# A two-mixer transformer layer on one core: five modulation groups in front, the context ahead of two gates, four modulation quarters brought forward

## The chip, the cores and the metric

The kernel runs as one program on one core of a Trainium2 chip. The metric is the device time of one execution in microseconds (us), the median of several runs. TensorE (PE) does the matrix products and transposes, VectorE (DVE) and ScalarE (ACT) the elementwise work, GpSimd (POOL) and SyncE (SP) mostly issue transfers. Each engine works through its own instructions in the order in which the program puts them; a semaphore holds an instruction back until what it reads is there and what it overwrites is free.

## What is computed

One layer over 512 latent tokens and 256 context tokens of width 1024, all in float32. What matters here is its beginning:

```python
m_lat = silu(c) @ mod_w + mod_b          # 6 sections of 1024: sh1, sc1, g1, sh2, sc2, g2
m_ctx = silu(c_ctx) @ mod_w + mod_b
h_lat = rms_norm(x,   norm_mix_g) * (1 + sc1)  + sh1
h_ctx = rms_norm(ctx, norm_mix_g) * (1 + csc1) + csh1
...
z_lat, z_ctx = h_lat @ w_in, h_ctx @ w_in   # qkv, decay and beta columns, gates g_a, g_b, m_a, m_b
...
x = x + g1 * ((sigmoid(m_a) * ya + sigmoid(m_b) * yb) @ w_out)
x = x + g2 * swiglu(rms_norm(x, norm_ffn_g) * (1 + sc2) + sh2)
```

Between the two places stand two token mixers (a gated delta rule and HGRN2), each run in both directions over context and latent tokens in chunks of 64. The front of the kernel, on which the change lies, makes `h_lat` and `h_ctx`, 8 of the 24 gate tiles, and the decay columns.

## The kernel before

**Products.** Each float32 operand is split in a high and a low part of a rounded type: `split` loads a weight tile `raw`, ScalarE writes `hi` (L100), VectorE writes `lo` (L102). A product is three matmuls, high by high, low by high and high by low (`mm3`, L110). `hhi`, `hlo` hold `h_lat` so, transposed (8 feature tiles of 128 features by 512 tokens), `chi`, `clo` hold `h_ctx` (by 256 tokens).

**The front, stage by stage** (all of it inside the pool `s1`). SP loads four tiles of x, then the first two sections of `mod_w`, 8 MB, as eight tiles `mw` of 1 MB (a ring of six buffers); after each two of them come two tiles `wr`, the weights of six gates for one feature tile, 384 KB each; then the two context tiles. Rows of x are normed (`norm_rows`, ACT L264, DVE L270).

- `modulation(q)`, q = 0 to 3, makes shift and scale of two feature tiles: PE multiplies the two `mw` tiles into `pmod` (L279, 16 matmuls in strips of 32 rows), DVE copies it to `mr` (L282), PE adds the strips and turns rows into columns with `comb` (L284, 128x2 matmuls), DVE adds biases into `mcol` (L291 to L293).
- `prepare(d)` calls `normed(d, 0, ...)`: PE transposes x into `px` (L299), ACT writes `hhi` (L301) and the unrounded `hf` (L303), DVE `hlo` (L304). Around it ACT writes `wh` (L313) and DVE `wl` (L315), the split of `wr`; they use the ring of two buffers that `hi` and `lo` use.
- Then 18 matmuls per feature tile (L330), 144 in all, add up the six gates 16 to 21 in six banks of PSUM, the accumulator memory of PE, named `pg` in the rows.
- `gate_out` copies a gate to `gt` (ACT, L136, two buffers) and writes it to memory (`gdram`, on SP). Gates 22 and 23 follow as ordinary products (`pgate`, 48 matmuls), then the eight context tiles (`normed(d, 1, ...)`, in the three PSUM banks of the tag "ga"), then small columns and the mask `lev`, loaded as float32 and cast by ACT (L346).
- The next block (pool `s3`) multiplies both streams by the decay columns (`pab`, L375), copies to `abT` (L376), transposes back (L379), and runs a row of some 25 small DVE steps from `ab` (L381) to `la` (L412), which PE sums into `pg` (L419) and ACT turns into `dec` (L422).

**The planner.** Everything after that comes from generators that emit work in the order of a string, `PLAN`: `H0` to `H3` and `G0`, `G2` are the parts of the two mixers, `F` emits one of the remaining gates, `N` and `aT` call `mod_early`. That function makes one quarter (256 columns) of one of the last three sections needed for `g1`, `sh2`, `sc2`: a transfer of 1 MB into a tile `mwe` on POOL's queue (L847), two multiplications (L851), six multiply-adds (L853), one addition (L854) on DVE, eight matmuls that sum the columns into `pmo` (L116), and an addition into `vc` (L862). Seven of the twelve are emitted so; four of these stand near the start of `PLAN`. In the rows, `h_z` are H0's projections, `g_k_zl`, `g_k_zc`, `g_q_zl`, `g_v_zl`, `g_v_zc` those of G0.

**What orders the instructions.** A scheduler places each instruction by a priority that counts up in program order; work emitted at a raised `tc.cur_priority` is filled in where the engine would otherwise stand. The resulting order on each engine is fixed when the program is built.

## Time and profile before

| | |
|---|---|
| median of 3 runs | 1079.61 us (1078.65 to 1081.12) |
| the profiled execution | 1081.61 us, its span 1079.6 us |
| granted PE clock, mean | 0.99 |
| time from the start to the end of the 144 gate matmuls | 70.4 us |
| time to the first matmul of G0 | 104.5 us |
| transfers | 122.07 MB, mean 113 GB/s |

The profile shows one execution. A row of a timeline reads: start, duration, engine, line, operation, what it writes and reads, shapes, number of instructions; in brackets stand the idle time of that engine just before it and what ended it. Durations of matmuls overlap, since the next one starts before the last has drained, so what one costs is read from the distance of starts.

### The profile page before, as it was taken

How to read it: one execution, taken by the hardware profiler on the slowest of the kernel's cores; microseconds unless marked ns; L12 is line 12 of the kernel's file. 1: busy time of each engine (PE TensorE's matmuls, PEld its weight loads, DVE VectorE, ACT ScalarE, POOL GpSimd, SP SyncE). 2: the span in 40 equal slices, each digit the busy share in tenths (PEclk: the TensorE clock that was granted, in tenths of full speed). 3: DMA queues.
4: the chain of work that ended last, by engine and by line, in shares of the span. 5: the costliest groups of instructions: out<-in, count | busy, mean ns of one | idle time of the engine just before them, and what ended most of it. 6: DMA issues, size and time to landing. Idle time of an engine off the chain costs nothing.

```text
span 1079.6 us, 16501 instructions
## 1 busy us (share of the span) xinstructions
PE 1014.1 (94%) x6455; PEld 839.9 (78%) x6455; DVE 656.5 (61%) x1238; ACT 554.5 (51%) x1042; POOL 76.6 (7%) x133
## 2 busy tenths in 40 slices
PE   4999999979999999999999899999999999999996
PEld 2686788858897877789777688797888878888785
DVE  3336886789867967976797565776343433422524
ACT  3456578748976765887774643442222222221212
POOL 1010000320002022000201000010000000000000
PEclk8999999999999999999999999999999999999999
DMA  9953412122004213200738743455333323322222
GB/s 329 290 168 91 138 55 65 54 79 59 3 11 147 64 45 88 59 2 22 241 112 280 239 159 120 137 158 174 98 97 96 96 85 98 97 97 96 86 95 95
DMA packets 134529, 122.07 MB, mean 113 GB/s; under 512 B 5533, under 2 KB 110259, under 8 KB 134451
## 3 DMA queue, kind: packets, MB, share of 16 engines
q1 hardware_dynamic: 127715, 100.20, 29.9%
q0 software_dynamic: 4640, 17.30, 4.9%
q10 hardware_dynamic: 2096, 3.50, 0.9%
q8 instruction: 51, 0.84, 0.3%
q14 instruction: 27, 0.22, 0.1%
HBM read 110.51 MB, written 10.49 MB: 112 GB/s over the span
## 4 chain that ended last, share of the span: by engine, by line
PE 60%; DVE 13%; DMA 9%; ACT 7%; issue 7%; POOL 3%; SPq 0%; POOLq 0%; ACTq 0%; DVEq 0%
PE pf L110 20%; PE pfo L110 10%; PE pg L330 3%; PE pup L110 3%; PE h_z L110 3%; PE pgate L110 2%; DMA mwb<-in_mod_w_dram 2%; DVE lo L102 2%; DMA mwe<-in_mod_w_dram 2%; PE h_zv L110 2%; DMA ug<-gdram 1%; ACT hi L100 1%; DMA gdram<-gt 1%; PE p_s_pk L801 1%; PE g_k_zl L110 1%
## 5 line engine op out<-in xcount | busy, mean ns | idle before, releaser
L100 ACT CAST hi<-raw 128x1024 fp32r<-128x1024 f32 (+1 forms) x131 | 129.7, 991 | 279.9 <-PE pf L110 97.3
L102 DVE TENSOR_TENSOR lo<-raw,hi 128x1024 fp32r<-128x1024 f32 (+1 forms) x131 | 150.5, 1150 | 172.6 <-ACT hi L100 172.2
L110 PE MATMUL pf<-hhi,lo 128*128 128x512 f32 (+1 forms) x352 | 133.8, 380 | 0.8 <-DVE lo L102 0.8
L110 PE MATMUL pf<-hhi,hi 128*128 128x512 f32 (+1 forms) x352 | 133.8, 381 | 0.0
L110 PE MATMUL pf<-hlo,hi 128*128 128x512 f32 (+1 forms) x352 | 133.7, 380 | 0.0
L110 PEld LDWEIGHTS pf<-hhi,lo 128*128 128x128 f32 x352 | 66.2, 188 | 13.7 <-DVE lo L102 1.2
L110 PEld LDWEIGHTS pf<-hlo,hi 128*128 128x128 f32 x352 | 66.2, 188 | 12.5 <-DVE hlo L1042 0.2
L110 PEld LDWEIGHTS pf<-hhi,hi 128*128 128x128 f32 x352 | 66.1, 188 | 12.5
L110 PE MATMUL pfo<-lo,uh 128*128 128x512 f32 x176 | 68.8, 391 | 0.1
L110 PE MATMUL pfo<-hi,ul 128*128 128x512 f32 x176 | 68.5, 389 | 0.0
L110 PE MATMUL pfo<-hi,uh 128*128 128x512 f32 x176 | 67.9, 390 | 0.0
L110 PE MATMUL pgate<-hhi,lo 128*128 128x512 f32 x144 | 59.2, 412 | 6.5 <-DVE lo L102 6.5
L110 PE MATMUL pgate<-hhi,hi 128*128 128x512 f32 x144 | 59.2, 411 | 2.3 <-ACT hi L100 2.3
L110 PE MATMUL pgate<-hlo,hi 128*128 128x512 f32 x144 | 58.2, 404 | 0.0
L1098 DVE TENSOR_TENSOR sg<-sg,pf 128x512 f32<-128x512 f32 x22 | 15.1, 687 | 49.3 <-PE pf L110 49.3
L835 DVE SCALAR_TENSOR_TENSOR acc<-mwb,sc,acc 128x256 f32<-128x256 f32 x72 | 34.5, 484 | 12.4 <-DMA mwb<-in_mod_w_dram 11.2
L110 PEld LDWEIGHTS pfo<-lo,uh 128*128 128x128 f32 x176 | 33.0, 188 | 7.8 <-DVE lo L102 1.0
L110 PEld LDWEIGHTS pfo<-hi,uh 128*128 128x128 f32 x176 | 32.8, 188 | 7.4 <-ACT hi L100 0.7
L110 PEld LDWEIGHTS pgate<-hhi,lo 128*128 128x128 f32 x144 | 27.8, 193 | 13.8 <-DVE lo L102 8.9
L110 PE MATMUL h_z<-hhi,hi 128*128 128x512 f32 x96 | 38.1, 397 | 0.4 <-ACT abT L376 0.3
L110 PEld LDWEIGHTS pfo<-hi,ul 128*128 128x128 f32 x176 | 33.0, 188 | 6.8
L110 PE MATMUL h_z<-hhi,lo 128*128 128x512 f32 x96 | 38.0, 396 | 0.0
(443 smaller groups left out, 2498.3 us busy)
## 6 DMA issues: line engine op xcount, KB each, us to landing
raw<-in_ffn_w_in_dram SPq DMA_DIRECT2D x44, 512.0 KB, 3.7
raw<-in_w_in_dram SPq DMA_DIRECT2D x37, 512.0 KB, 3.7
raw<-in_ffn_w_out_dram SPq DMA_DIRECT2D x22, 512.0 KB, 3.6
mwb<-in_mod_w_dram POOLq DMA_DIRECT2D x18, 512.0 KB, 4.6
mw<-in_mod_w_dram SPq DMA_DIRECT2D x16, 512.0 KB, 6.0
mwe<-in_mod_w_dram POOLq DMA_DIRECT2D x7, 1024.0 KB, 6.1
gdram<-gt SPq DMA_DIRECT2D x24, 256.0 KB, 3.3
...
```

The lines of the kernel that those rows point to most:

```text
L100: nc.scalar.copy(hi[:, :, :], raw[:, :, :])
L102: nc.vector.tensor_tensor(lo[:, :, :], raw[:, :, :], hi.bitcast(F32), op=ALU.subtract)
L110: nc.tensor.matmul(ps, a[u](k), b[v](k), start=(start and n == 0), stop=(stop and n == tot - 1))
L330: nc.tensor.matmul(pg0[i][:, :], u[:, P * i:P * i + P], v[:, d, :], start=(d == 0 and n == 0), stop=(d == KT - 1 and n == 2))
L801: nc.tensor.matmul(pk[:, 2 * P:3 * P], kend[:, :], u[:, :], start=True, stop=True)
L835: nc.vector.scalar_tensor_tensor(acc[:, :], mw[:, k - k0, :], sc[:, k:k + 1], acc[:, :], op0=ALU.mult, op1=ALU.add)
L1098: nc.vector.tensor_tensor(sg[:, :], sg[:, :], pgu[1][:, :], op=ALU.mult)
```

## The change

1. **Five groups.** `modulation` takes a range of feature tiles: (0,1), (1,2), (2,4), (4,6), (6,8). The first two groups need one `mw` tile of 1 MB each (all 1024 rows, 128 columns of each section, so runs of 512 bytes instead of 1 KB). `wr0` is loaded behind the first `mw`, `wr1` behind the second. The column matmuls go in strips of 32 columns (32x2, four times as many).
2. **The context first.** `normed(d, 1)` follows the six gates directly, in the two banks "ha"; of every odd tile `hf` is written by DVE.
3. **Fillers.** Gates 22 and 23 and four quarters (`mwe20` to `mwe23` by the numbers in the rows below) are emitted at a priority raised by 1500. The gates get own tiles `rw` for their high and low parts, the quarters tiles of the ring `mw`, loaded on SP. The four entries at the start of `PLAN` go; the other `N` and `aT` stay and use POOL as before.
4. **Small.** `lev` is passed as bytes (112 KB loaded in place of 448 KB, no cast). `gt` has three buffers in the front.

```diff
-PLAN = ("H0:1 aT:1 N:1 aT:2 G0:6 F:1 H1:3 G0:4 F:1 G2:3 G0:5 F:2 N:1 G0:1 H0:2 "
+PLAN = ("H0:1 G0:6 F:1 H1:3 G0:4 F:1 G2:3 G0:5 F:2 N:1 G0:1 H0:2 "
...
-    return sq, np.concatenate(lev, axis=1).astype(np.float32)
+    return sq, np.concatenate(lev, axis=1).astype(np.uint8)
...
-            gt = pool.tile([P, SEQ], F32, name=f"gt{i}", tag=tag, bufs=2)
+            gt = pool.tile([P, SEQ], F32, name=f"gt{i}", tag=tag, bufs=3 if pool is ring.get("sp") else 2)
...
+        quarters = [(sec, j) for sec in (2, 3, 4) for j in range(4)]
+
+        def mod_now(sec, j, mw, queue):
+
+            c0 = D * sec + 256 * j
+            queue.dma_start(mw[:, 0:KT, :], T["mod_w"][0, :, c0:c0 + 256].rearrange("(k p) f -> p k f", p=P))
+            for k in range(KT):
+                acc = mw[:, k % 2, :]
+                if k < 2:
+                    nc.vector.tensor_scalar_mul(acc, acc, sc[:, k:k + 1])
+                else:
+                    nc.vector.scalar_tensor_tensor(acc, mw[:, k, :], sc[:, k:k + 1], acc, op0=ALU.mult, op1=ALU.add)
+            nc.vector.tensor_tensor(mw[:, 0, :], mw[:, 0, :], mw[:, 1, :], op=ALU.add)
+            mod_sum(sec, j, mw[:, 0, :], "fa")
+
+        def mod_sum(sec, j, acc, tag):
+            ps = bank(tag, f"pmo{sec}{j}")
+            for i in range(2):
+                column_sums(ps, i, acc[:, P * i:P * i + P])
+            c = 8 * sec + 2 * j
+            nc.vector.tensor_tensor(mbc[:, c:c + 2], ps[:, 0:2], mbc[:, c:c + 2], op=ALU.add)
...
+            groups = ((0, 1), (1, 2), (2, 4), (4, 6), (6, 8))
+
+            def load_mod(d0, d1):
+                n, kn = P * (d1 - d0), KT // (d1 - d0)
+                for k0 in range(0, KT, kn):
+                    mw = s1.tile([P, kn, 2 * n], F32, name=f"mw{d0}_{k0}", tag="mw", bufs=6)
+                    for j in range(2):
+                        c0 = D * j + P * d0
+                        nc.sync.dma_start(mw[:, :, n * j:n * j + n],
+                                          T["mod_w"][0, P * k0:P * (k0 + kn), c0:c0 + n].rearrange("(k p) f -> p k f", p=P))
+                    for k in range(kn):
+                        mws.setdefault(d0, []).append(mw[:, k, :])
...
+            wrs = [s1.tile([P, NG0 * P], F32, name="wr0", tag="wr", bufs=5)]
+            for g in (0, 1):
+                xts[g] = s1.tile([P, D], F32, name=f"xt{g}")
+            for d0, d1 in groups:
+                load_mod(d0, d1)
+                for e in range(d0, d1):
+                    wr = wrs.pop() if wrs else s1.tile([P, NG0 * P], F32, name=f"wr{e}", tag="wr", bufs=5)
                     nc.sync.dma_start(wr[:, :], W_IN[P * e:P * e + P, C_MB:C_MB + NG0 * P])
                     wraws.append(wr)
-                if d == 1:
+                if d0 == 1:
...
+            def modulation(d0, d1):
+
+                nd = d1 - d0
+                ps = bank("ha", f"pmod{d0}")
+                for k, mw in enumerate(mws[d0]):
+                    r = slice(32 * (k % 4), 32 * (k % 4) + 32)
+                    nc.tensor.matmul(ps[r, 0:2 * P * nd], sch[:, k, :], mw, start=(k < 4), stop=(k >= 4), tile_position=(0, r.start))
+                mr = s1.tile([P, 512], F32, name=f"mr{d0}", tag="mr", bufs=2)
+                nc.vector.tensor_copy(mr[:, 0:2 * P * nd], ps[:, 0:2 * P * nd])
+                for i in range(2 * nd):
+                    for j in range(0, P, 32):
+                        nc.tensor.matmul(ps[j:j + 32, 2 * i:2 * i + 2], mr[:, P * i + j:P * i + j + 32], comb[:, :],
+                                         start=True, stop=True, tile_position=(0, j))
+                col = ps[:, 0:4 * nd].rearrange("p (j d s) -> p j s d", j=2, s=2)
+                dd = slice(d0, d1)
...
+                if s == 1 and d % 2:
+                    nc.vector.tensor_scalar(hf[:, 0:n], px[:, 0:n], scl, sh, op0=ALU.mult, op1=ALU.add)
+                else:
+                    nc.scalar.activation(hf[:, 0:n], px[:, 0:n], AF.Identity, bias=sh, scale=scl)
...
-            modulation(0)
+            modulation(*groups[0])
             prepare(0)
+            nxt = {0: 1, 1: 2, 2: 3, 4: 4}
             for d in range(KT):
-                if d % 2 == 0 and d + 2 < KT:
-                    modulation(d // 2 + 1)
+                if d in nxt:
+                    modulation(*groups[nxt[d]])
                 if d + 1 < KT:
                     prepare(d + 1)
...
-            for i in rest[0:2]:
-                gate(i, sp)
             for d in range(KT):
-                normed(d, 1, (0, 1), chi, clo, "ga")
+                normed(d, 1, (0, 1), chi, clo, "ha")
...
-            levf = s1.tile([P, 7 * P], F32, name="levf")
-            nc.sync.dma_start(levf[:, :], T["lev"])
-            nc.scalar.copy(lev[:, :], levf[:, :])
+            nc.sync.dma_start(lev[:, :], T["lev"])
...
+            tc.cur_priority += 1500
+            for i in rest[0:2]:
+                w = [s1.tile([P, KT, P], F32R, name=f"rw{i}{j}") for j in range(2)]
+                w = split([W_IN[:, gcols[i]:gcols[i] + P]], KT, P, dst=[t[:, :, :] for t in w])
+                gate_out(i, feat(w, lat, SEQ, f"pgate{i}"), sp, "gt")
+            for q in quarters[0:4]:
+                mod_now(*q, s1.tile([P, KT, 256], F32, name="mwe%d%d" % q, tag="mw", bufs=6), nc.sync)
+            del quarters[0:4]
+            tc.cur_priority -= 1500
...
+            mod_now(sec, j, gd.tile([P, 12 if tag == "N" else KT, 256], F32, name=f"mwe{sec}{j}", tag=tag), nc.gpsimd)
```

The tensors' numbers in the rows that follow tell instances apart (`px01` is feature tile 1 of x, `px12` tile 2 of the context). On PE, around the first gate matmuls, before:

```order
L279 MATMUL pmod0_216<-mw1_117,sch_181 32x512 x4
L299 MATMUL px00_237<-sq_91,xt5_112 128x128
L284 MATMUL pmod0_216<-comb_184,mr0_225 128x2 x4
L330 MATMUL pg0_0_210<-hhi_73,wh0_234 128x512
L330 MATMUL pg0_1_211<-hhi_73,wh0_234 128x512
L330 MATMUL pg0_2_212<-hhi_73,wh0_234 128x512
L330 MATMUL pg0_3_213<-hhi_73,wh0_234 128x512
L330 MATMUL pg0_4_214<-hhi_73,wh0_234 128x512
L330 MATMUL pg0_5_215<-hhi_73,wh0_234 128x512
L330 MATMUL pg0_0_210<-hhi_73,wl0_235 128x512
```

and in the changed kernel:

```order
L315 MATMUL pmod0_216<-comb_184,mr0_225 32x2 x8
L310 MATMUL pmod1_251<-mw1_0_121,sch_181 32x256 x8
L366 MATMUL pg0_0_210<-hhi_73,wh0_238 128x512
L331 MATMUL px01_276<-sq_91,xt2_106 128x128
L331 MATMUL px01_276<-sq_91,xt3_108 128x128
L331 MATMUL px01_276<-sq_91,xt4_110 128x128
L331 MATMUL px01_276<-sq_91,xt5_112 128x128
L315 MATMUL pmod1_251<-comb_184,mr1_260 32x2 x8
L366 MATMUL pg0_1_211<-hhi_73,wh0_238 128x512
L366 MATMUL pg0_2_212<-hhi_73,wh0_238 128x512
```

The first group no longer stands behind `mw1`; the second group's matmuls and the transposes of feature tile 1 now stand ahead of and right behind the first gate matmul.

On ACT, from the first to the fourth feature tile, before:

```order
L301 ACTIVATE hhi_73<-px01_268,mcol_189 128x512
L303 ACTIVATE hf01_274<-px01_268,mcol_189 128x512
L313 CAST wh2_296<-wr2_134 128x768
L301 ACTIVATE hhi_73<-px02_299,mcol_189 128x512
L303 ACTIVATE hf02_305<-px02_299,mcol_189 128x512
L313 CAST wh3_345<-wr3_136 128x768
L301 ACTIVATE hhi_73<-px03_348,mcol_189 128x512
```

and in the changed kernel:

```order
L333 ACTIVATE hhi_73<-px01_276,mcol_189 128x512
L338 ACTIVATE hf01_282<-px01_276,mcol_189 128x512
L348 CAST wh2_334<-wr2_136 128x768
L348 CAST wh3_395<-wr3_138 128x768
L333 ACTIVATE hhi_73<-px02_337,mcol_189 128x512
L338 ACTIVATE hf02_343<-px02_337,mcol_189 128x512
L333 ACTIVATE hhi_73<-px03_398,mcol_189 128x512
```

The cast `wh3` now stands ahead of `hhi` of tile 2, where it stood behind it and `hf`.

On DVE, from the copy `ab2` of the decay columns on, before:

```order
L381 COPY ab2_758<-pab_751 128x192
L388 COPY cw_765<-pr_762 128x60
L383 TENSOR_TENSOR ab_760<-ab2_758 128x96
L390 COPY dta_767<-pr_762 128x16
L241 TENSOR_SCALAR beta_796<-ab_760 128x48
L395 TENSOR_TENSOR zz_772<-ab_760,dta_767 128x48
L393 TENSOR_SCALAR nal_769<-nal_769 128x8
L397 SCALAR_TENSOR_TENSOR e_774<-zz_772 128x48
```

and in the changed kernel:

```order
L424 COPY ab2_902<-pab_895 128x192
L162 TENSOR_SCALAR mwe23_832<-mwe23_832,sc_173 128x256
L426 TENSOR_TENSOR ab_904<-ab2_902 128x96
L162 TENSOR_SCALAR mwe23_832<-mwe23_832,sc_173 128x256
L438 TENSOR_TENSOR zz_916<-ab_904,dta_911 128x48
L271 TENSOR_SCALAR beta_940<-ab_904 128x48
L164 SCALAR_TENSOR_TENSOR mwe23_832<-mwe23_832,sc_173 128x256
L440 SCALAR_TENSOR_TENSOR e_918<-zz_916 128x48
L273 TENSOR_SCALAR beta_940<-beta_940 128x48
L164 SCALAR_TENSOR_TENSOR mwe23_832<-mwe23_832,sc_173 128x256
L443 TENSOR_SCALAR t_921<-e_918 128x48
L452 TENSOR_SCALAR zz_916<-zz_916 128x48
```

Between the small steps that lead to `la` there now stand the eight steps of quarter `mwe23`.

## Rows read from the trace of the kernel before

**Rows 1.** Page, part 1: busy us (share of the span) xinstructions of each engine.

```profile
PE 1014.1 (94%) x6455; PEld 839.9 (78%) x6455; DVE 656.5 (61%) x1238; ACT 554.5 (51%) x1042; POOL 76.6 (7%) x133
```

**Rows 2.** Stretches: us, busy (x) of PE, PEld, DVE, ACT, POOL; clock, DMA share, GB/s.

```profile
20.00:24.00 4.00, 2.58 (x6) 2.10 (x7) 2.05 (x4) 1.45 (x2) 0.00 (x0) 0.50 1.10 358
...
52.00:56.00 4.00, 4.00 (x27) 3.02 (x20) 1.75 (x6) 1.65 (x3) 0.55 (x1) 1.00 0.01 4
```

**Rows 3.** Timeline of PE in the front (columns as told above).

```profile
13.25 1.93 PE L279 MATMUL pmod<-mw,sch 128*32 128x512 f32 x8 [7.43 <-DVE xt L270]
...
16.22 1.20 PE L279 MATMUL pmod<-mw,sch 128*32 128x512 f32 x8 [0.21 <-DMA mw<-in_mod_w_dram]
...
21.42 2.93 PE L330 MATMUL pg<-hhi,wh 128*128 128x512 f32 x6 [2.13 <-ACT hhi L301]
...
27.75 1.06 PE L279 MATMUL pmod<-mw,sch 128*32 128x512 f32 x8
...
30.27 0.97 PE L330 MATMUL pg<-hhi,wh 128*128 128x512 f32 x3 [0.40 <-ACT hhi L301]
...
33.36 0.96 PE L284 MATMUL pmod<-comb,mr 128*128 128x2 f32 x8
...
37.00 1.07 PE L330 MATMUL pg<-hhi,wh 128*128 128x512 f32 x4
...
69.03 1.52 PE L330 MATMUL pg<-hlo,wh 128*128 128x512 f32 x6
```

**Rows 4.** Timeline of ACT in the front.

```profile
34.88 0.78 ACT L301 ACTIVATE hhi<-px,mcol 128x512 fp32r<-128x512 f32 x1 [3.27 <-DVE mcol L293]
...
37.20 0.83 ACT L313 CAST wh<-wr 128x768 fp32r<-128x768 f32 x1 [0.87 <-PE pg L330]
...
74.17 1.24 ACT L136 COPY gt<-pg 128x512 f32<-128x512 f32 x2 [2.52 <-DMA gdram<-gt]
```

**Rows 5.** Timeline of PE, rest gates, context and decay columns.

```profile
70.39 0.39 PE L110 MATMUL pgate<-hhi,hi 128*128 128x512 f32 x1
...
81.28 0.81 PE L299 MATMUL px<-sq,xt 128*128 128x128 f32 x6
...
83.27 0.31 PE L375 MATMUL pab<-chi,wab 128*32 128x256 f32 x1 [1.02 <-ACT chi L301]
...
100.69 0.60 PE L419 MATMUL pg<-la,sq 128*128 128x24 f32 x4
...
104.50 0.40 PE L110 MATMUL g_k_zl<-hhi,hi 128*128 128x512 f32 x1
```

**Rows 6.** Timeline of DVE, the chain from the decay columns to `la`.

```profile
94.71 0.36 DVE L381 COPY ab<-pab 128x192 f32<-128x192 f32 x1 [0.75 <-PE pab L379]
...
100.34 0.20 DVE L412 TENSOR_TENSOR la<-e,nal 128x48 f32<-128x48 f32 x1
```

**Rows 7.** Timeline of PE in G0's projections.

```profile
128.34 0.31 PE L116 MATMUL pmo<-ones,mwe 128*32 128x1 f32 x16 [1.69 <-DVE mwe L854]
...
130.83 0.63 PE L110 MATMUL pgate<-hhi,hi 128*128 128x512 f32 x1
...
132.54 0.43 PE L110 MATMUL pgate<-hlo,hi 128*128 128x512 f32 x1
```

**Rows 8.** Stretches of PE: us, busy (x), granted clock, DMA share, GB/s.

```profile
130.00:131.00 1.00, 1.00 (x6) 0.50 0.00 0
...
200.00:260.00 60.00, 53.42 (x346) 0.97 0.24 68
```

**Rows 9.** Tile `mwe`, whole run: ns min/median/max, first and last start; landing times.

```profile
L853 DVE SCALAR_TENSOR_TENSOR mwe<-mwe,sc x42: 477/480/484, 100.7 to 524.1; 128x256 f32<-128x256 f32 x42
...
DMA to landing us min/median/max: 5.6/6.1/7.9
```

**Rows 10.** Page, part 6: transfers, KB each, median us from issue to landing.

```profile
raw<-in_ffn_w_in_dram SPq DMA_DIRECT2D x44, 512.0 KB, 3.7
...
raw<-in_ffn_w_out_dram SPq DMA_DIRECT2D x22, 512.0 KB, 3.6
```

53 lines of the change are left out of this document (5 added, 48 removed).

## The prediction

> **What bounds the kernel.** The page's busy shares come first [rows 1]: PE is busy for 94% of the span, DVE for 61%, ACT for 51%. So time goes only where PE works less, waits less, or runs at the full one of its two clock levels (2.4 GHz) instead of half (1.2 GHz). The change keeps nearly all of PE's work; what it can win are PE's idle and half-clock stretches in the first 135 us, which the timelines of PE, ACT and DVE show. The stretches [rows 2] show that transfers are the limit only at the start: from 20 to 24 us the DMA engines are full at 358 GB/s while PE is busy 2.58 of 4 us at a granted clock of 0.50, the lower level; from 52 to 56 us 4 GB/s move while PE is busy throughout at 1.00. Later than about 22 us the front waits for PE's own stream.
>
> The sum is made against the profiled execution (1081.61 us, span 1079.6, so 2.0 us lie around the span). It is 2.0 us above the median of the runs, 1079.61; that difference is taken off at the end.
>
> **Part 1, five groups.** In the trace `mw1` ends PE's wait at 16.22, the column matmuls, `mcol` and `hhi` follow, and the first gate matmul starts at 21.42, after 2.13 us of idle [rows 3]. Now the first group needs `mw0` alone, which PE has at 13.25 [rows 3]. But the order of PE puts the second group's matmuls and transposes around the first gate matmul; they need the second megabyte, now behind `wr0`. 384 KB at 358 GB/s [rows 2] are 1.1 us, so that megabyte lands near 17.2 instead of 16.1. Matmuls (1.2 us), copy, transposes and column matmuls bring PE to about 20.0 for the other 17 gate matmuls. Gain 1.4 us.
>
> From there, 16 gate matmuls took 21.42 to 27.75 [rows 3], 0.40 each at mostly half clock; 17 of them end feature tile 0 near 27.0, where the trace has 30.27 (with half a group, transposes and 0.40 us of idle between). Tile 1 then holds 18 matmuls at 0.23 (6 in 1.36 at 69.03 to 70.39, [rows 3, 5]), both halves of the next group (1.06 each), transposes and column matmuls: 7.2 us, end at 34.2, where the trace has 37.00.
>
> Here a new stall appears. ACT's order puts the cast `wh3` ahead of `hhi` of tile 2. `wh` has two buffers, so `wh3` waits until PE has finished tile 1; in the trace `wh3` comes after `hhi` and waits for PE too [rows 4], which costs nothing there. Now PE waits for 0.83 (`wh3`) plus 0.78 (`hhi`) [rows 4] plus some 0.15 of signalling, 1.75 us. Tile 2 starts at about 35.9 against 37.0: of 2.8 us gained 1.1 are left.
>
> The column matmuls in strips: 8 took 0.96, about 0.8 from start to start [rows 3]. The strips have no row. Nearest is the row of 128x1 strips, 16 in 0.31 [rows 7], by which 16 would cost 0.3 to 0.4. The upper bound is no gain. I take 0.35 gained in each of the two groups behind the stall, 0.7. So the 144 matmuls end 1.8 us earlier, at about 68.6; the bounds are 0 (a second such stall) and 3.5 (none).
>
> What the transfers cost: the rows have 512 KB in 512-byte runs (`ffn_w_in`) landing in 3.7 us and in longer runs (`ffn_w_out`) in 3.6 [rows 10], so I add nothing for the shorter runs. The Trainium skill ("DMA: Bandwidth & Descriptors", section "Why small descriptors are slow") charges each small piece a fixed overhead; by it, an estimate of mine is that 512-byte runs move about 9% slower than 1 KB runs, 0.25 us per group. By that the front would gain 1.2 instead of 1.4.
>
> **Part 2, context and rest gates.** From the end of the 144 matmuls (70.39) to the first matmul of G0 (104.50) the trace has 34.1 us [rows 5]. 48 `pgate` matmuls fill 70.39 to 81.28, 0.227 each; then the context's tiles go at ACT's pace, with idle like the 1.02 before 83.27, and `la` at 100.34 frees the sums at 100.69 [rows 5, 6]. In the new order the transposes stand among the gate matmuls, which cover ACT's chain. PE's work to the copy `ab2`: 42 gate matmuls 9.5, 16 transposes 2.2, the decay columns 5.5, transposes back and small pieces 1.0, waits of 0.5: 18.7 us. Then comes the chain to `la`: 94.71 to 100.54 in the trace, 5.8 [rows 6], and the eight steps of `mwe23` now stand in it: six at 0.48 [rows 9] at a pitch of 0.41 and two cheaper ones, about 3.3 in all. So `la` is there 27.9 after the start, while PE has run out of other work at about 25.6 and idles 2.3. Sums 1.4, 24 context matmuls 2.9 and two column sums 0.5 bring it to 33.0: gain 1.1. Bounds: 0 loss of cover gives 3.4, and an `mwe23` that lands late takes it all (rival D).
>
> **Part 3, four quarters out of G0's projections.** From 104.50 to the first `pgate` there (130.83, [rows 5, 7]) are 26.3 us for 72 matmuls at 0.227 and 48 of half the width at half of that, 22 us. The 4.2 above that are four `pmo` insertions, among them the wait of 1.69 for DVE [rows 7], and the lower clock after that wait: 0.50 from 130 to 131 us [rows 8]. Four `pgate` matmuls at 130.83 to 132.54 [rows 7] take 1.71 instead of 0.91, 0.8 more. Without quarters there it is 5.0 less. PE will then reach the norm sums of G0 before ACT and DVE have finished the convolution; I give back 0.7. Gain 4.3; bounds 2.5 (the wait moves to the next item of that chain) and 5.0.
>
> **Costed at nothing.** The cast of `lev` (ACT is idle for PE there) and the third `gt` buffer (ACT's wait of 2.52 for `gdram`, [rows 4], lies beside PE's gate matmuls); if ACT had no slack, they would be gains of a us each. SP's queue carries 4 MB more, in the window in which it moves 4 GB/s [rows 2]. POOL's queue is relieved. DVE's 32 quarter steps fall into its idle time under the 144 matmuls and the gate matmuls, except those of part 2.
>
> Sum: 1.8 + 1.1 + 4.3 = 7.2. 1081.6 - 7.2 = 1074.4 for that execution; less 2.0, **1072.4** for the median.
>
> **Rivals.**
>
> *A, forecast:* gain 4.5 to 9.5, 1070.1 to 1075.1.
>
> *B, DVE's relief carries on.* In 200 to 260 us PE is busy 53.42 of 60 us [rows 8], so 6.6 are idle; if the earlier start and the shifted order spare half of that, 3.3 to 5 more: 1067 to 1069. For it: the changed order differs far behind the front. Against: those waits belong to the mixers' own chains, which the change does not touch.
>
> *C, idle brings the lower clock.* Two new idle stretches stand in the sum, 1.75 and 2.3 us. After 1.69 us of idle the trace has the clock at 0.50 [rows 7, 8], and that cost PE about 1.6 us there: 0.8 in the four `pgate` and, since 16 column sums and 12 half-width matmuls took 128.34 to 130.83, 2.5 for 0.3 + 12 x 0.12 = 1.7, 0.8 ahead of them. If both do the same, 3.2 are lost: gain 4.0, 1075.6. Against: after 0.40 of idle at 30.27 the matmuls went on at a pace of 0.23 [rows 3], and each of the two new stalls is a sum of small terms that may come out shorter. The Trainium skill ("TensorE: Matmul & The Clock Gate", section "HAM oscillation") has an idle PE fall back to half clock; by it this case is the likelier one for the longer stall.
>
> *No change:* the gain comes in front and is given back at G0's chains, whose ACT and DVE steps keep their length: 1077.4 to 1081.8.
>
> *D, slower.* One mechanism: `mwe23` on SP stands behind the write of gate 22, which waits for ACT's copy of that gate. I put its issue at about 11.6 us after the 144 matmuls and, with 6.1 to 7.9 of landing [rows 9], its arrival at 17.7 to 19.5, just where DVE's first step on it (18.7) stands ahead of `ab`. Each us later delays `la` and so PE by one. Some 5.6 us late, with the lower clock behind the wait, cancels the gain; this decides from an arrival at 26 on, 14 us from issue to landing. With 10 us late it is 1083. Against: the longest landing is 7.9.
>
> **How the numbers follow.** A .47, B .11, C .22, no change .11, D .09. What a measurement of this kernel can tell from no change is 0.2%, 2.2 us. A, B and C lie beyond it on the fast side, .80; no change .11; slower .09. The range from 1066.0 to 1078.0 takes in A, B and C with the terms' bounds (0 to 3.5, 0 to 3.4, 2.5 to 5.0) and leaves D and most of no change out.
>
> **What would show it.** In the profile after: the first `pg` matmul of the row of 17 near 20.0; an idle stretch of PE of 1.75 ended by `hhi` at tile 2; the last `pg` matmul ending near 68.6; the context's transposes among `pgate` without waits above 0.5; `la` some 28 us after that, PE idle ahead of its sums; the first G0 projection at about 101.6; no `pmo` among G0's projections, which run 22 us at clock 1.00. It would be wrong if PE's idle before the sums is above 5 us with `mwe23`'s transfer as its end, or if the wait ahead of the norm sums `g_k_pn` is above 3 us.

## The result: slower, and the profile after

The changed kernel takes 1084.64 us (median of 6 runs, 1083.87 to 1085.85), the kernel before 1080.01 in the same comparison (6 runs, 1078.65 to 1081.62). The ratio is 1.0043, interval 1.0030 to 1.0056: 4.6 us slower, where 1072.4 was forecast. The profiled execution of the changed kernel took 1084.9 us, its span is 1083.2.

The page's busy times after, to be held against [rows 1]:

```profile
PE 1018.9 (94%) x6567; PEld 843.8 (78%) x6567; DVE 659.3 (61%) x1246; ACT 549.2 (51%) x1037; POOL 72.4 (7%) x129
```

PE's busy time grew by 4.8 us with 112 matmuls more, small ones of the modulation, while the mean granted clock fell from 0.990 to 0.983. Idle time did not grow: the span less PE's busy time is 65.5 us before and 64.3 after. More of PE's work ran at the lower clock. One measure takes idle time and clock together. I call **lost time** of a stretch its length less PE's busy time times its granted clock, and sum it over all stretches of 5 us (210 rows of the stretches view per kernel, to 1050 us). It is rough: it counts the column strips as full work, misses work at half pace where the granted clock reads 1.00 (last section), and comes from one execution per kernel. The profiled executions of runs 5, 7 and 10 are the fastest of their kernels, some 3 us below the median, that of run 1 is the slowest, 5.0 above. Differences of 2 or 3 us in it mean little. Cumulated, in us:

```
up to                 140   200   300   400   500   540   580   620   1050
before               26.4  28.0  38.5  42.4  48.7  50.9  54.6  58.6   63.5
the change           19.9  19.9  35.5  38.8  44.3  50.3  57.6  64.1   68.0
e1_groups            24.0  25.2  37.2  43.6  49.6  51.8  55.4  59.0   65.5
e2_nogroups          17.3  17.4  32.0  35.4  42.2  48.0  55.7  61.2   66.0
e3_noq               30.3  31.3  47.1  50.0  56.8  63.2  69.8  71.1   83.0
e4_no_late_n         19.5  19.5  35.9  38.9  44.7  47.1  57.3  64.1   68.3
e5_pin_after_front   20.6  21.4  32.0  37.2  42.6  46.3  49.2  52.5   56.0
e6_pin_before_front  31.8  35.0  49.4  52.2  57.7  62.2  68.2  71.3   83.6
e7_quarters_yield    19.7  19.8  35.7  40.4  45.6  50.8  60.1  66.0   71.7
e8_pin_late          19.7  19.8  36.3  39.6  45.9  49.9  54.4  56.1   61.8
e9_pin_early         18.7  19.6  30.1  37.5  42.8  46.7  50.8  55.1   59.5
e10_pin_mid          18.7  19.6  30.1  35.7  41.1  45.1  48.0  50.9   54.8
e11_pin_mid_wh       17.5  18.3  29.3  34.4  40.1  45.9  51.1  53.7   59.4
e12_edge             18.0  18.1  34.5  37.3  43.2  46.4  51.8  59.0   62.6
```

At 200 us the changed kernel leads by 8.1 us, close to the 7.2 of the sum. It then gives back 5.1 between 200 and 300 us, and 9.9 between 500 and 620 us (19.8 lost there against 9.9). At 620 us it is 5.5 behind. The front did what was forecast, and the time went where the change edits nothing.

The start of one and the same matmul in both kernels tells more about the two give-backs. `p_s_pk` takes the steps of the delta rule in PSUM, `pwo` is the product with `w_out`, which stands behind both mixers. From the tile views (count, ns min/median/max, first and last start), before and after:

```profile
L810 PE MATMUL p_s_pk<-p_s_r,p_aT x64: 271/275/377, 300.1 to 512.7; 128*128 128x128 f32 x64
L110 PE MATMUL pwo<-hi,mh x32: 389/389/389, 652.2 to 673.3; 128*128 128x512 f32 x32
```

```profile
L853 PE MATMUL p_s_pk<-p_s_r,p_aT x64: 270/275/377, 295.7 to 505.7; 128*128 128x128 f32 x64
L110 PE MATMUL pwo<-hi,mh x32: 389/389/389, 656.2 to 677.3; 128*128 128x512 f32 x32
```

At its last `p_s_pk` (505.7) the changed kernel is still 7.0 us ahead. So the 5.1 that lost time shows between 200 and 300 us did not hold the delta rule back by as much; what it costs in the end is not shown. From there to the first `pwo` it takes 150.5 us where the kernel before takes 139.5, and is then 4.0 behind. The loss lies there: 11.0 us, most of them the lost time of 500 to 620 us.

**The front.** PE's timeline of the changed kernel (start, length, line and operation, count; in brackets the idle time ahead and what ended it):

```profile
13.90 1.94 PE L310 MATMUL pmod<-mw,sch 128*32 128x256 f32 x16 [8.36 <-DMA mw<-in_mod_w_dram]
18.51 1.94 PE L310 MATMUL pmod<-mw,sch 128*32 128x256 f32 x16 [1.09 <-DMA mw<-in_mod_w_dram]
22.05 1.43 PE L366 MATMUL pg<-hhi,wh 128*128 128x512 f32 x5
23.31 1.52 PE L366 MATMUL pg<-hhi,wl 128*128 128x512 f32 x6
...
35.33 2.50 PE L366 MATMUL pg<-hhi,wh 128*128 128x512 f32 x5 [1.64 <-ACT hhi L333]
...
68.34 1.52 PE L366 MATMUL pg<-hlo,wh 128*128 128x512 f32 x6
69.70 0.60 PE L331 MATMUL px<-sq,xt 128*128 128x128 f32 x4
...
102.38 0.50 PE L110 MATMUL g_k_zl<-hhi,hi 128*128 128x512 f32 x1 [0.20 <-ACT h_Z L512]
...
125.57 0.58 PE L116 MATMUL g_k_pn<-ones,g_k_acc 128*32 128x1 f32 x48
```

The second megabyte lands at 18.5, not 17.2, so the row of 17 gate matmuls starts at 22.05 instead of 20.0. It then runs faster than forecast, five matmuls in 1.26 us from start to start. The stall of 1.75 before tile 2 is there, 1.64 long and ended by `hhi`. What follows the gate matmuls starts at 69.70, against 70.39 [rows 5]. From there to G0's first projection it takes 32.7 (34.1 before), and from the projection to the norm sums 23.2 instead of 29.1 (104.50 to 133.60): 5.9 less, at a clock of 1.00 from 102 to 132 us.

**500 to 620 us.** Five stretches of the changed kernel (stretch, its length, PE busy and its instructions, granted clock, share of the DMA engines, GB/s):

```profile
500.00:520.00 20.00, 16.70 (x111) 0.91 0.46 157
520.00:540.00 20.00, 20.00 (x120) 0.92 0.74 225
540.00:560.00 20.00, 18.17 (x103) 1.00 0.45 145
560.00:580.00 20.00, 15.83 (x92) 0.91 0.47 146
...
600.00:620.00 20.00, 15.29 (x60) 0.91 0.65 217
```

and of the kernel before:

```profile
500.00:520.00 20.00, 19.70 (x126) 1.00 0.43 146
520.00:540.00 20.00, 18.10 (x127) 1.00 0.70 212
540.00:560.00 20.00, 19.35 (x121) 1.00 0.41 130
560.00:580.00 20.00, 16.96 (x103) 1.00 0.60 189
...
600.00:620.00 20.00, 15.97 (x69) 1.00 0.70 227
```

Before, PE keeps the clock at 1.00 in all five; after, it falls to 0.91 or 0.92 in four of them. The first fall can be followed step by step. The timelines of POOL, DVE, ACT and PE of the changed kernel:

```profile
505.03 0.96 POOL L158 DMA_DIRECT2D mwe<-in_mod_w_dram  x1 [8.49 <-PE p_s_pk L835]
513.76 2.67 POOL L475 TENSOR_TENSOR p_hs<-p_hs,mhalf 128x4 f32<-128x4 f32 x1 [5.82 <-DVE p_hs L474]
```

```profile
511.00 0.62 DVE L162 TENSOR_SCALAR mwe<-mwe,sc 128x256 f32<-128x256 f32 x2 [4.26 <-DMA mwe<-in_mod_w_dram]
511.53 2.06 DVE L164 SCALAR_TENSOR_TENSOR mwe<-mwe,sc 128x256 f32<-128x256 f32 x5
513.51 0.16 DVE L474 SCALAR_TENSOR_TENSOR p_hs<-p_hs,g_vec 128x4 f32<-128x4 f32 x1
...
521.76 0.95 DVE L518 SCALAR_TENSOR_TENSOR h_K<-h_Z,h_sg 128x768 f32<-128x768 f32 x1
```

```profile
516.46 1.28 ACT L477 ACTIVATE p_on<-p_oa,p_hs 128x128 f32<-128x128 f32 x4 [3.33 <-POOL p_hs L475]
```

```profile
516.91 0.48 PE L480 MATMUL p_pt<-sq,p_on 128*128 128x128 f32 x1 [3.30 <-ACT p_on L477]
```

and PE's stretches around it:

```profile
510.00:515.00 5.00, 3.61 (x16) 1.00 0.75 262
515.00:520.00 5.00, 3.09 (x24) 0.65 0.33 106
520.00:525.00 5.00, 5.00 (x28) 0.66 0.78 252
```

POOL issues the transfer of the late quarter `mwe31` at 505.03, when PE's `p_s_pk` lets it. DVE, which works in order, has seven steps of that quarter ahead of `p_hs` of the second head pair, and nothing else to do before them. It stands 4.26 us until the megabyte is there. `p_hs` runs at 513.51, then POOL, then ACT (3.33 us of idle), then PE (3.30 us of idle). Around that wait the clock is 0.65 and 0.66; by the three stretches 1.4, 3.0 and 1.7 us are lost, 6.1 of 15. H2's `h_sg` stands behind the same ACT step, and five steps of the next quarter, `mwe32`, stand on DVE ahead of H2's first `h_K`, which comes at 521.76.

In the kernel before the same `p_hs` also stands behind `mwe31`, issued at 512.01. But there DVE has H2's first steps ahead of the quarter, which fill most of the flight. Its timeline, and PE's:

```profile
514.00 0.96 DVE L475 SCALAR_TENSOR_TENSOR h_K<-h_Z,h_sg 128x768 f32<-128x768 f32 x1 [0.24 <-ACT h_sg L473]
518.18 0.62 DVE L851 TENSOR_SCALAR mwe<-mwe,sc 128x256 f32<-128x256 f32 x2 [1.75 <-DMA mwe<-in_mod_w_dram]
```

```profile
523.01 0.62 PE L437 MATMUL p_pt<-sq,p_on 128*128 128x128 f32 x2 [1.90 <-ACT p_on L434]
```

DVE waits 1.75 and PE 1.90, and H2 is already under way. The two programs of DVE at this place, before:

```
L431 SCALAR_TENSOR_TENSOR p2_hs0<-p2_hs0,g2_vec 128x4
...
L475 SCALAR_TENSOR_TENSOR h2_K<-h2_Z0,h2_sg0 128x768
L102 TENSOR_TENSOR lo40<-raw40,hi40 128x512
L476 SCALAR_TENSOR_TENSOR h2_sg0<-h2_Z0,h2_sg0 128x768
L851 TENSOR_SCALAR mwe31<-mwe31,sc 128x256 x2
L853 SCALAR_TENSOR_TENSOR mwe31<-mwe31,sc 128x256 x6
L431 SCALAR_TENSOR_TENSOR p2_hs1<-p2_hs1,g3_vec 128x4
```

and after:

```
L474 SCALAR_TENSOR_TENSOR p2_hs0<-p2_hs0,g2_vec 128x4
...
L162 TENSOR_SCALAR mwe31<-mwe31,sc 128x256 x2
L164 SCALAR_TENSOR_TENSOR mwe31<-mwe31,sc 128x256 x5
L474 SCALAR_TENSOR_TENSOR p2_hs1<-p2_hs1,g3_vec 128x4
...
L518 SCALAR_TENSOR_TENSOR h2_K<-h2_Z0,h2_sg0 128x768
```

No line of `mwe31`, `p_hs` or H2 was edited. The order on each engine is fixed when the program is built, by the scheduler and its own estimates, and the edit in front changed it far behind the front.

**200 to 240 us** shows the same kind of loss on a smaller scale. ACT, changed kernel:

```profile
220.19 1.05 ACT L100 CAST hi<-raw 128x1024 fp32r<-128x1024 f32 x1 [3.99 <-PE g_v_zc L110]
```

and PE, the gate and the stretches around it:

```profile
224.30 0.50 PE L110 MATMUL pgate<-hhi,hi 128*128 128x512 f32 x1 [3.10 <-ACT hi L100]
```

```profile
225.00:230.00 5.00, 4.61 (x44) 0.66 0.35 101
```

The cast of a rest gate's weights (128x512, at 223.64) stands five instructions behind one that waits 3.99 us for PE; PE reaches that gate, finds no weights and idles 3.10, and the clock behind is 0.66. Before, a wait of 2.89 for `lo` stands at the corresponding place, so this place is worse but not new, and by the starts above it has cost little of the lead at 505 us.

### The profile page after: what moved, and what is told of

The parts are those of the page before. It is cut to its first block, busy times and chain, and to the rows that moved or that the text cites. A ratio compares the mean times of both kernels' runs of the same rounds, so it can differ in the third digit from the quotient of the medians.

```text
span 1083.2 us, 16716 instructions
## 1 busy us (share of the span) xinstructions
PE 1018.9 (94%) x6567; PEld 843.8 (78%) x6567; DVE 659.3 (61%) x1246; ACT 549.2 (51%) x1037; POOL 72.4 (7%) x129
## 4 chain that ended last, share of the span: by engine, by line
PE 43%; DVE 4%; DMA 4%; issue 3%; ACT 3%; POOL 1%; SPq 0%; POOLq 0%; ACTq 0%; DVEq 0%
PE pf L110 22%; PE pfo L110 10%; PE pup L110 3%; DMA uy<-ydram 1%; PE pgate L110 1%; PE pwo L110 1%; PE h_pA L531 1%; DMA mwb<-in_mod_w_dram 1%; DVE lo L102 1%; ACT hi L100 1%; PE p_s_pk L835 1%; PE p_s_pk L844 1%; DVE acc L878 0%; DMA ug<-gdram 0%; PE h_z L110 0%
## 5 line engine op out<-in xcount | busy, mean ns | idle before, releaser
L102 DVE TENSOR_TENSOR lo<-raw,hi 128x1024 fp32r<-128x1024 f32 (+1 forms) x129 | 148.0, 1147 | 171.0 <-ACT hi L100 170.6
L110 PEld LDWEIGHTS pf<-hhi,hi 128*128 128x128 f32 x352 | 66.1, 188 | 12.3
L110 PE MATMUL pgate<-hhi,hi 128*128 128x512 f32 x128 | 52.9, 413 | 4.1 <-ACT hi L100 4.0
L110 PE MATMUL pgate<-hhi,lo 128*128 128x512 f32 x128 | 52.4, 410 | 4.3 <-DVE lo L102 4.3
L110 PE MATMUL pgate<-hlo,hi 128*128 128x512 f32 x128 | 51.9, 405 | 0.0
L878 DVE SCALAR_TENSOR_TENSOR acc<-mwb,sc,acc 128x256 f32<-128x256 f32 x72 | 34.4, 480 | 9.9 <-DMA mwb<-in_mod_w_dram 8.6
L110 PE MATMUL h_z<-hlo,hi 128*128 128x512 f32 x96 | 39.0, 406 | 0.0
```

What stands on the lines that cost most here:

```text
L102: nc.vector.tensor_tensor(lo[:, :, :], raw[:, :, :], hi.bitcast(F32), op=ALU.subtract)
L110: nc.tensor.matmul(ps, a[u](k), b[v](k), start=(start and n == 0), stop=(stop and n == tot - 1))
L878: nc.vector.scalar_tensor_tensor(acc[:, :], mw[:, k - k0, :], sc[:, k:k + 1], acc[:, :], op0=ALU.mult, op1=ALU.add)
```

## The experiments

Two theories stood against each other from the first run on. **O**: the order that the scheduler gives the later stages takes the gain back, so the front with another order behind it keeps it. **B**: the middle is bound by ACT, DVE and late transfers, whatever the order; it hands any early gain back. The kernel before was timed beside each set; its medians there are 1082.29 (runs 1 to 4), 1081.64 (5 to 7), 1083.21 (8 to 11) and 1081.76 (12). Runs of different sets are compared by their ratios to it.

Which order a kernel got can be read from the traces, by the sequence of an engine's instructions (operation, tile and shape). What is said of orders below rests on the computing instructions of DVE, ACT and POOL from 170 us on, 2000 in the kernel before.

**1, e1_groups**: the kernel before with the five groups alone (the parts of the diff on `modulation`, `load_mod` and the order of loads; `PLAN`, context, `lev` and `gt` as before).

> Part 1 alone: the kernel before with the five modulation groups, everything else as before. Let lost time be what PE was idle or ran below the full clock, summed from the start. Theory O (the order written for the later stages takes the gain): the last of the 144 matmuls ends at 69.7 as in the change (70.4 before), PE has lost about 0.7 us less than before at 200 us, and what follows differs from before by either sign, up to 5 us, because the order is written anew. Theory B (the middle of the kernel is bound by ScalarE, VectorE or transfers and hands back whatever the front gains): the total is that of before within 1 us.

Measured: 1081.01, ratio 0.9989 (0.9976 to 1.0002). The last gate matmuls start at 69.05, so the 144 matmuls end where they ended before; 2.8 us of lead at 200 us are gone at 400. The groups alone give nothing that can be measured. They do not rewrite the order either, as theory O had it: from 170 us on it is that of the kernel before. So the 18.4 us lost from 200 to 400 us, 14.4 before, are no effect of an order; this is the slowest execution of ten.

**2, e2_nogroups**: the change without the five groups.

> Parts 2 to 4 without part 1: modulation in four groups of two as before, the context ahead of the rest gates, gates and four quarters as fillers. Theory O: the 144 matmuls end at 70.4, PE has lost about 7 us less than before at 200 us, and the total lies anywhere between 1073 and 1086 with the order that results. Theory B: lost time returns to that of before or above by 620 us, total 1080 to 1085.

Measured: 1085.06, ratio 1.0014 (0.9993 to 1.0035). It has the largest lead at 200 us of the first four (10.6), and is 2.6 behind at 620. Neither a lead nor its size shows in the end. From 170 us on its order is that of the change, so it is parts 2 to 4 that brought the new order.

**3, e3_noq**: the change with its four early quarters back at the head of `PLAN`.

```diff
-PLAN = ("H0:1 G0:6 F:1 H1:3 G0:4 F:1 G2:3 G0:5 F:2 N:1 G0:1 H0:2 "
+PLAN = ("H0:1 aT:1 N:1 aT:2 G0:6 F:1 H1:3 G0:4 F:1 G2:3 G0:5 F:2 N:1 G0:1 H0:2 "
...
-            for q in quarters[0:4]:
-                mod_now(*q, s1.tile([P, KT, 256], F32, name="mwe%d%d" % q, tag="mw", bufs=6), nc.sync)
-            del quarters[0:4]
```

> The change with the four quarters put back at the head of the plan (POOL's queue, tiles of the mixers' pool); groups, context first and filler gates stay. Both theories: pmo insertions and a wait for VectorE return among G0's projections, so the lost time at 200 us is 3 to 4 us below before's instead of 8. Theory O: the total is then not bound to be above the change's, 1076 to 1086. Theory B: the total is that of before within 1 us, and if the front quarters themselves do the harm later, this kernel is faster than the change by 3 to 5 us.

Measured: 1098.6, ratio 1.0134 (1.0102 to 1.0165), outside both expectations. It loses 11.4 us more than the change up to 200 us, and at 1050 us it has lost 15.0 more. The four quarters were costed at 4.3 us in part 3; what the other 7 up to 200 us are was not traced. From 170 us on the order is that of the change, so the order there does not explain the difference.

**4, e4_no_late_n**: the change, with the late quarters in the tail of `PLAN` (`N:1`, `aT:1`) left to their normal late place, so that `mwe31` and `mwe32` are not in the way at 505 us.

```diff
-        "F:1 G0:99 H0:99 F:3 G2:4 H1:99 G2:4 F:1 G2:99 N:1 H3:99 aT:1 H2:1 X H2:99")
+        "F:1 G0:99 H0:99 F:3 G2:4 H1:99 G2:4 F:1 G2:99 H3:99 H2:1 X H2:99")
```

> The change without the two last early quarters (N:1 ahead of H3:99 and aT:1 behind it); these two join the late quarters. In the change VectorE stands 4.26 us at 506.7 for the transfer of the first of them, seven of its steps stand ahead of p_hs, p_on follows at 516.46, PE is idle 3.30 and at the lower clock until about 527, and H2's chain starts 8 us later than before. Theory O: with those steps gone p_on starts 3 to 4 us sooner, h_K of H2 at about 514, and the lost time between 500 and 540 us falls from 6.0 to about 2; the total is 1079 to 1081. Theory B: the chain from 500 to 600 us is bound by VectorE's work as such, and more quarters late (12 more VectorE steps under the same load) make it 1084 to 1086.

Measured: 1084.72, ratio 1.0028 (1.0011 to 1.0045). The place itself was healed, 2.4 us lost from 500 to 540 instead of 6.0, but 540 to 580 lost 10.2 instead of 7.3 and at 620 the sum is the change's again. Place and lost time to 540 came out as in O, the total as in B. But from 505 us on the order had been rewritten once more, so the run could not decide.

**5, e5_pin_after_front**: the change's front, and from the decay columns on the order of the kernel before on every engine, for the 7312 instructions that both kernels have. The edges bind two instructions of one engine and add no wait between engines:

```diff
+    for k in ORDER:
...
+        if last is not None:
+            tc.add_manual_dep(insts[k], last.name, mybir.DependencyInfo(mybir.DependencyClass.NoSync, mybir.DependencyReason.DATA), reason="order")
+        last = insts[k]
```

> The change's front with before's order behind it: from the decay columns on, all 7312 instructions that the two kernels share stand on each engine in the order of the kernel before (an ordering edge without a semaphore from each to the next); nothing is removed. Theory O (the new order of the later stages takes the gain): the front's lead of 7 to 8 us at 200 us stays, the lost time at 620 us is 5 to 9 us below before's, the total is 5 to 9 us below before's, near 1073. Theory B (the middle is bound by ScalarE, VectorE or transfers and hands back what the front gains): the lead is gone by 620 us, the total is that of before within 2 us or above.

Measured: 1077.04, ratio 0.9962 (0.9945 to 0.9980). The lead is 6.6 at 200 us and 6.1 at 620, and the profiled span is 1072.3 against 1079.6. Its stretches, where the change lost most:

```profile
500.00:520.00 20.00, 17.67 (x116) 1.00 0.46 160
520.00:540.00 20.00, 18.67 (x120) 1.00 0.80 236
540.00:560.00 20.00, 19.17 (x118) 1.00 0.31 105
560.00:580.00 20.00, 17.88 (x101) 1.00 0.78 248
```

The clock stays at 1.00 in all four, and from 500 to 620 us 9.9 are lost, as before. The same front, the same work, another order behind: 1.0043 against 0.9962, some 9 us between the two kernels. By the medians this one is 4.6 us below the kernel before. That is outside what B allowed (2 us) and just short of what O expected (5 to 9); the profile, of the fastest of ten executions, makes it look larger. So the order takes more than the whole gain, and some of the 7.2 of the sum is missing even without it.

**6, e6_pin_before_front**: the reverse, the front of before with the change's order behind it.

> The reverse: before's front and quarters, and behind them, from the decay columns on, the change's order of the 7312 shared instructions. Theory O: the front has no lead and the order costs what it cost the change between 200 and 620 us, 10 to 13 us more than before's own order: total 1087 to 1094. Theory B: the stretches that hand back a lead have none to hand back, total 1079 to 1083.

Measured: 1099.58, ratio 1.0181 (1.0149 to 1.0213). Worse than O expected: 7.0 us more than before are already lost at 200 us, perhaps because the change's order behind the decay columns was made for a front that ends earlier and has done other work, which was not tested. From 200 to 620 us it loses 36.3, before 30.6, but its stages come later than in the other kernels, and fixed stretches cut them elsewhere. From the last `p_s_pk` to the first `pwo` it takes 150.4 us, as long as the change, though it is 8.2 us behind the kernel before when that stretch begins. Theory B has no lead there to hand back; the order costs the same without one. From 200 to 1050 us it loses 13.1 more than before, close to O's 10 to 13.

**7, e7_quarters_yield**: the change, the three early quarters that remain in `PLAN` given a later priority.

```diff
+            tc.cur_priority += 3000
             mod_now(sec, j, gd.tile([P, 12 if tag == "N" else KT, 256], F32, name=f"mwe{sec}{j}", tag=tag), nc.gpsimd)
+            tc.cur_priority -= 3000
```

> The change with the three remaining early quarters emitted at a priority raised by 3000, so that their VectorE steps stand behind H2's h_K and p_hs comes earlier among them. Nothing is removed, no work is added late. Theory O: H2's chain starts before the quarters, lost time from 500 to 580 us falls from 13.3 us in the change to 6 to 8 (before had 5.9), and the total to 1076 to 1080. Theory B: lost time from 500 to 620 us stays at 18 to 20, total 1083 to 1086.

Measured: 1089.45, ratio 1.0090 (1.0059 to 1.0121): a miss. From 500 to 580 us 14.5 are lost, 13.3 in the change. The order differs from the change's from 328 us on: a priority moves more than the instruction it is given to.

**8, e8_pin_late**, and **9, e9_pin_early**: as run 5, with the order of before held only behind, or only up to, the place that the profile of before reaches at some 410 us.

> The change with before's order only for the instructions that stand behind about 410 us in before; up to there its own order. In the change 500 to 620 us lose 19.8 us of PE's time, in before and in the kernel with the whole order of before 9.9. Theory O, the loss sits in the late order: lost time at 400 us as in the change (38.8), from 500 to 620 us about 10, total 8 to 10 us below the change and 4 to 6 below before. If the earlier places (212 to 240, 265 to 285 us) carry the loss, the total stays within 3 us of the change.

> The reverse half: before's order up to about 410 us, behind it the order that the scheduler writes. Theory O with the loss in the late order: lost time at 400 us 37 to 38, as with the whole order of before (37.2), then 15 to 20 us lost from 500 to 620 us, total 1080 to 1086. If the early places carry the loss: 10 us there and a total of 1074 to 1077.

Measured: 1078.87, ratio 0.9965 (0.9942 to 0.9989), and 1079.05, ratio 0.9954 (0.9930 to 0.9979). Run 8 lost 19.8 us between 200 and 400 us, before its pin begins (the change 18.9, before 14.4), but only 10.2 from 500 to 620: the late order of before is enough to bring the kernel under the one before. Run 9 lost 10.5 from 200 to 300, as before and not 15.6 as the change, and missed behind it: I had expected the change's 15 to 20 us from 500 to 620, it lost 12.3. Behind its pin the scheduler, though free, wrote the order of before again: on DVE, ACT and POOL the sequence is that of run 5 from start to end. So run 9 is run 5 measured once more (0.9962 and 0.9954; 9.9 and 12.3 lost from 500 to 620). It shows that the late order follows from the early one, and nothing about the late order's price. What the early order costs by itself stays open: run 8, which keeps it, can't be told from runs 5 and 9.

**10, e10_pin_mid**: the change's own order up to G0's first norm sums, the order of before behind them. **11, e11_pin_mid_wh**: the same and, for the stall found in front, an order on ACT that keeps each cast `wh` of tile 3 and up behind `hf` of the tile before it:

```diff
+    for d in range(3, KT):
...
+        tc.add_manual_dep(wh, hf.name, mybir.DependencyInfo(mybir.DependencyClass.NoSync, mybir.DependencyReason.DATA), reason="order")
```

> The change up to the first norm sums of G0 (its own order of the decay columns, H0 and G0's projections), behind them before's order to the end. With before's order from the decay columns on, 21.4 us were lost at 200 us, with the change's own order there 19.9. Theory O: 20 us lost at 200 us, the rest as with the whole order of before, total 1 to 2 us below that kernel (1077.0), the fastest so far. Theory B: no lead left at 620 us, total 1080 or more.

> As the kernel before it in this list, and on ScalarE the cast of wh of tile d (d from 3 on) stands behind hf of tile d-1, as it does in before; that takes away the wait of 1.64 us at 35.33 in the change and the lower clock behind it (0.66 from 34 to 38 us). If the wait is what kept part 1 from gaining, the 144 matmuls end 1.6 to 2.5 us sooner than in the change (its last row of them starts at 68.34), and the total is 1.5 to 2.5 us below the kernel before it in this list. If the transfers of the next groups are the limit, another wait of 1 to 2 us appears and the end stays.

Measured: 1078.48, ratio 0.9953 (0.9930 to 0.9977), and 1076.88, ratio 0.9925 (0.9901 to 0.9950). PE's timeline of run 10, around the stall and at the end of the 144 matmuls:

```profile
37.16 1.43 PE L434 MATMUL pg<-hhi,wh 128*128 128x512 f32 x5 [1.64 <-ACT hhi L401]
...
68.66 1.52 PE L434 MATMUL pg<-hlo,wh 128*128 128x512 f32 x6
```

and of run 11:

```profile
34.35 1.65 PE L437 MATMUL pg<-hhi,wh 128*128 128x512 f32 x6 [0.54 <-ACT hhi L404]
...
65.80 1.52 PE L437 MATMUL pg<-hlo,wh 128*128 128x512 f32 x6
```

Five edges on ACT take the stall from 1.64 to 0.54 and end the 144 matmuls 2.9 us earlier than in run 10, 2.5 earlier than in the change. Run 11 is faster than both kernels and has the lowest median of all. Run 10 can't be told from run 5, and the intervals of 10 and 11 overlap; what is beyond doubt is the earlier end of the matmuls.

**12, e12_edge**: the change as it is, with one rule: on DVE the steps of `mwe31` and `mwe32` come behind the second `p_hs` and H2's first `h_K` and `h_sg`.

```diff
+    quarter = steps("mwe31_") + steps("mwe32_")
+    for i in quarter:
+        for j in steps("p2_hs1_")[-1:] + steps("h2_K_")[:1] + steps("h2_sg0_")[:1]:
+            tc.add_manual_dep(i, j.name, mybir.DependencyInfo(mybir.DependencyClass.NoSync, mybir.DependencyReason.DATA), reason="order")
```

> The change with one ordering edge at the place that the trace shows at 507 to 522 us: on VectorE the steps of the two quarters mwe31 and mwe32 stand behind p_hs of the second pair of heads and behind H2's first h_K and h_sg; no other edge, nothing removed, nothing late added. If the place is what its rows say (VectorE held 4.26 us for mwe31's transfer with p_hs and H2 behind it), p_on starts 2 to 3 us sooner than 516.46, PE's idle of 3.30 ahead of p_pt falls to about 1.5 and the clock stays up, 500 to 540 us lose 2 to 3.5 us instead of 6.0, and, since H2's chain starts 4 to 5 us sooner, 540 to 620 us lose less than the 13.8 us of the change: total 3 to 8 us below the change, within 3 us of before. If the loss only moves on, as when the quarters were left out there, 540 to 620 us lose 14 to 17 us and the total is the change's within 2 us.

Measured: 1079.97, ratio 0.9987 (0.9966 to 1.0008); the change's is 1.0043. DVE and PE of run 12:

```profile
512.71 0.17 DVE L474 SCALAR_TENSOR_TENSOR p_hs<-p_hs,g_vec 128x4 f32<-128x4 f32 x1 [0.61 <-ACT p_on L470]
517.39 0.96 DVE L518 SCALAR_TENSOR_TENSOR h_K<-h_Z,h_sg 128x768 f32<-128x768 f32 x1 [4.52 <-ACT h_sg L516]
```

```profile
514.49 0.33 PE L480 MATMUL p_pt<-sq,p_on 128*128 128x128 f32 x1 [0.27 <-ACT p_on L477]
```

PE's wait ahead of `p_pt` falls from 3.30 to 0.27 and H2's `h_K` comes 4.4 us earlier. From 500 to 540 us 3.2 are lost, not 6.0; from 540 to 620 us 12.6, not 13.8. Edge and scheduler cannot be parted fully here either: the order is the change's up to 511 us, and from there to some 620 us more has moved than the steps named. Part of the shorter chain is POOL's step on `p_hs`, 1.03 us here and 2.67 in the change. But the chain of 500 to 527 us is what it was meant to be, and 4 us of the loss hang on it, 5.0 by the starts (145.5 us from `p_s_pk` to `pwo`).

**All runs by their order.** From the last start of `p_s_pk` to the first of `pwo`, and lost time from 200 to 1050 us:

| order from 170 us on | kernels | `p_s_pk` to `pwo`, us | lost, us |
|---|---|---|---|
| that of before | before, runs 1, 5, 9, 10, 11 | 139.5, 138.8, 139.2, 141.9, 139.2, 143.5 | 35.5, 40.3, 34.6, 39.9, 35.2, 41.1 |
| the change's, from about 400 us that of before | run 8 | 139.3 | 42.0 |
| that of the change | the change, runs 2, 3, 6 | 150.5, 149.4, 152.8, 150.4 | 48.1, 48.6, 51.7, 48.6 |
| the change's up to 328, 505 and 511 us, then another | runs 7, 4, 12 | 150.2, 149.9, 145.5 | 51.9, 48.8, 44.5 |

The first and the third row do not overlap. Front and order stand here in all four pairs: with the order of before 139.5 (front of before) and 139.2 (front of the change, run 5), with the order of the change 150.4 (run 6) and 150.5. What counts is the order, and not whether the kernel comes to the stretch ahead of the kernel before (the change by 7.0, run 11 by 8.2) or behind it (run 1 by 3.0, run 6 by 8.2).

## Why the prediction was wrong

- **Part 1, five groups (1.8).** 0.7 in the profiled execution. The second megabyte landed 1.3 us later than the 17.2 that I worked out from 384 KB at full rate, and the row of 17 began 2.05 later. The rate was not full. PE's stretches of the changed kernel and of the one before end in DMA share and GB/s:

```profile
9.00:18.00 9.00, 3.38 (x36) 1.00 1.13 316
```

```profile
9.00:18.00 9.00, 4.22 (x20) 1.00 1.08 363
```

  The DMA engines are as full as before and move 13% less, 0.42 MB in these 9 us or 1.2 us of transfer. From 14 to 16 us it is 296 to 302 GB/s in the eleven kernels that have the groups, and 368 to 376 in the three that have not (before, runs 2 and 6). The runs of 512 bytes are the likely reason, though the order of loads changed too. The sum added nothing for them; the 0.25 us per group that the prediction set beside it had the right sign and was too small. The late start was made good by luck: I had taken 0.40 us for each of the 17, at mostly half clock, and they went at some 0.23, so tile 2 began at 35.33, earlier than the 35.9 of the sum. The stall of 1.75 was right (1.64). What was mis-sized is the time behind it: 34.4 us to the end of the 144 matmuls, not 32.7. From 35 to 39 us the clock is 0.56 and 0.58, which loses 1.6 us, the price that rival C had for one stall and that the sum left out. Run 11, with a stall of 0.54, starts the last six 3.2 us earlier than before (65.80 against 69.03), within the bounds. Alone, the part gave nothing that can be told from no change (run 1).
- **Part 2, context and rest gates (1.1).** 1.4: 32.7 us against 33.0 forecast. The forecast's own terms (27.9, 1.4, 2.9, 0.5) add up to 32.7; 0.3 was lost in the addition. That the total fits is partly luck, as the two halves miss it by 1.6 us each way. DVE's two ends of the chain, changed kernel:

```profile
88.66 0.36 DVE L424 COPY ab<-pab 128x192 f32<-128x192 f32 x1 [0.51 <-PE pab L422]
...
96.03 0.20 DVE L455 TENSOR_TENSOR la<-e,nal 128x48 f32<-128x48 f32 x1
```

  `ab2` stands at 19.0 us after the 144 matmuls (18.7 forecast), `la` at 26.3 (27.9 forecast), and the idle of 2.3 us did not come. From `la` to G0's first projection it took 6.4 us, not 4.8.
- **Part 3, four quarters out (4.3).** Right in mechanism, low in size: 5.9 less between projection and norm sums. Of these some 1.1 are gate matmuls that now stand elsewhere (three there, eight before, at 0.227), so 4.8 are won. I had given back 0.7 for a wait at the norm sums; `g_k_pn` shows none.
- **Sum (7.2).** 8.1 by lost time at 200 us. To here the prediction holds.
- **The step that failed** is the next one, and it has no number in the prediction: "1081.6 - 7.2 = 1074.4", the sum at about 135 us carried to the end unchanged. The text said of the later stages that the changed order "differs far behind the front", and took this as a point for rival B, a gain. It should have been a term with two signs. Parts 2 to 4, edits in the first 135 us, rewrote the order of the next 500 (part 1 alone did not, run 1), and between 200 and 620 us the new order lost 44.2 us where the old one lost 30.6: 5.1 more up to 300 us, 1.4 less from there to 500, 9.9 more behind. The 13.6 are the 8.1 of the lead and the 5.5 by which the change is behind at 620. By the starts of `p_s_pk` and `pwo`, a lead of 7.0 us became 4.0 behind in one stretch, and every kernel with that order to its end took 149 to 153 us for it, not the 139 to 144 of the old order. Run 5 shows what the sum was worth with the old order behind the new front: 4.6 us by the medians, of 7.2 forecast (7.3 by the span of the one execution that was profiled).
- **Rival C, the lower clock at the new stalls.** Right for the first: after the stall of 1.64 the clock was 0.56 and 0.58 from 35 to 39 us, at the price that C had (1.6). The second stall was not there.
- **Rival D, slower.** It had the right mechanism at the wrong place: a quarter's transfer that lands late, with its steps ahead of a chain on DVE. `mwe23` landed in time; `mwe31` at 511 us did what D describes, on POOL's queue and not on SP's, and not because it came later than before but because nothing was left ahead of it to fill its flight. Its price there was 4 to 5 us (run 12), and D's chance of .09 was priced for one quarter of many.
- **No change** said that the gain would be given back at G0's chains, because ACT and DVE keep their length. The give-back at 200 to 300 us lies in that region, but by runs 5 and 9 it is the order and not the length: held, the loss is 10.6 and 10.5, as before.

What stays open: why the scheduler's estimates lead to just these orders, and which of parts 2 to 4 turned the one into the other (not the four quarters, which run 3 has at their old place); what cost run 3 its 11.4 and run 6 its 7.0 before 200 us; the other 6 us of the 11.0 behind the place of run 12; and the places at 212 to 240 and 265 to 280 us, which no run tried without the late ones.
